# One group of gate columns moved to seven-product form, with its factors made earlier and twelve low parts made by adding transfers

## The chip, the cores and the metric

The kernel runs on one core of a Trainium2 chip. Five engines each follow an instruction list of their own: TensorE (PE, matrix products, with PEld loading its weights), VectorE (DVE), ScalarE (ACT), GpSimd (POOL) and SyncE (SP). Transfers between the main memory and the on-chip memory are issued from the queues of SP, ACT or POOL. The metric is the device time of one execution in microseconds, lower is better. Times of the kernel before: 806.62 us, the median of 3 runs (806.59 to 807.14).

## The reference

One decoder layer over 512 tokens of width 1024, in float32: a norm, one wide projection, three attention branches side by side (banded attention, called SWA; stick-breaking attention, SB; attention over 256 memory rows, MEM), each multiplied by a sigmoid gate of its own, an output projection and a gated feed-forward block.

```python
u = rms_norm(h, ln_mix_pre[l])
proj = jnp.einsum('bsd,de->bse', u, w_in[l])
qa, ka, va, qb, kb, vb, qm, gl = jnp.split(proj, split_idx, axis=-1)
...
g = jax.nn.sigmoid(gl.reshape(B, S, N_BRANCH, D))
merged = (g[:, :, 0] * jnp.einsum('bse,ed->bsd', y_swa, w_branch_swa[l])
          + g[:, :, 1] * jnp.einsum('bse,ed->bsd', y_sb, w_branch_sb[l])
          + g[:, :, 2] * jnp.einsum('bse,ed->bsd', y_mem, w_branch_mem[l]))
```

What the change touches is `gl`, the gates: three branches of 1024 columns each, computed from the normed input `u` (1024 x 512, eight row blocks of 128).

## The kernel before

**Three products for one.** Every float32 operand is split into a rounded part `hi` and the rest `lo`, and a product of two operands is three matmuls into the same bank: hi·hi, hi·lo and lo·hi (`mm3`, L167, whose matmuls are L169, L171 and L172 in the profile). `split` (L132) makes the parts: ScalarE copies the raw weights to `hi` with rounding (L135), VectorE subtracts `hi` from the raw weights to get `lo` (L136). With a sign of -1, the same two steps are L138 and L139.

**A stream of units.** The weights come through a `Stream` (L33), a list of units of 512 KB each, in the order in which they were added. Loads run four units ahead of the products and splits three units ahead (`ahead`, L58). There are five `raw` tiles and four `hi` and four `lo` tiles for all units, so the split of a unit waits until TensorE has finished the unit four places earlier. `run(us)` (L92) issues products of the stream worth so many us by a cost that is written in the code, to fill the time in which an attention head waits for VectorE and ScalarE. `until(flag)` (L97) issues them up to a mark. The instructions get their priority from the order in which the program makes them, and the compiler lays out each engine's list by that priority, taking a later instruction where an earlier one is not ready. An engine then works its list in order.

**Plain and seven-product gates.** A plain unit (`proj`, L286) is one 128-column block of the projection: 8 row blocks x 3 matmuls of 512 columns, 24 in all. Four such blocks make a group of 512 columns, and a group can also be computed with seven products of half-size blocks in place of eight (`add_quarters`, L445, `quarter`, L428), in the order p1, p2, p5, p6, p3, p7, p4, each of 24 matmuls of 256 columns. Weights of the sums are made by transfers from POOL that add to a tile in place (`q_plus`, L375) and by additions on VectorE (`q_sum`, L390). The right-hand factors are combinations of the blocks of `u`: `rights` (L457) makes those of p6, p7 and p4, and `right_t1` (L482) writes the factor of p5 over the right half of the upper blocks of `u`, so that no plain unit may follow it. Results are put together in `q_end` (L397), and the sigmoids are taken in `sigmoids` (L333) and `gate_out` (L343).

**Order before.** After the eight stick-breaking heads and the SB gates (eight plain units, mark `gates1`), the list of units goes on: four `qm` units (queries of MEM), four SB branch units (`branch`, L583), four plain SWA gate units (columns 0, 1, 4, 5, tile `g`), the mark `plain_end`, seven products for the other SWA group, four SWA branch units, and 14 products for MEM. The driver (L990 to L1006) runs four pairs of banded heads over them, then the factors, then the memory heads:

```python
for c in range(4):
    for us in swa_pair(c, bias):
        dn.run(us)
for _ in rights():
    dn.run(2.0)
dn.until("plain_end")
right_t1()
dn.until(f"gates{SWA}")
```

A pair of banded heads (`swa_pair`, L878) is a chain: scores (`s`, 16 matmuls), then 10 us asked of the stream while VectorE and ScalarE do the softmax of `w`, then 14 transposes (`pt`), 2 us of the stream while `pts` is copied, 16 matmuls of values (`ysw`), and the split of the result into `y0ch` on ScalarE and `y0cl` on VectorE.

**Tiles.** `ck` (L118) hands out 68 tiles of 128 x 512 for nearly everything else. `dps` (L124) has two banks of the matmul memory and `aps` (L127) has six.

Of the kernel before, what the change touches and what calls it, by code (L numbers as in the profile page):

```python
# [32 lines left out]
class Stream:  # L33
# [12 lines left out]
    def add(self, src, n, mm):  # L46
        self.units.append({"src": src, "n": n, "mm": mm, "load": [], "split": [], "flags": []})

    def on_load(self, fn):
        self.units[-1]["load"].append(fn)  # L50

    def on_split(self, fn):
        self.units[-1]["split"].append(fn)

    def mark(self, flag):
        self.units[-1]["flags"].append(flag)

    def ahead(self, load_to, split_to):  # L58
        while self.loaded <= min(load_to, len(self.units) - 1):
            u = self.units[self.loaded]  # L60
            for fn in u["load"]:
                fn()
            u["raw"] = u["src"]() if callable(u["src"]) else self.load(u["src"], u["n"])
            self.loaded += 1
        while self.have <= min(split_to, len(self.units) - 1):
            u = self.units[self.have]
            for fn in u["split"]:
                fn()
            u["hl"] = self.split(u["raw"], u["n"])
            self.have += 1  # L70

    def later(self, us, fn):
# [18 lines left out]

    def run(self, us):  # L92
        self.owed += us
        while self.owed > 0 and self.at < len(self.units):
            self.owed -= self.piece()

    def until(self, flag):  # L97
# [6 lines left out]
def tile_kernel(ctx, tc, a):  # L104
# [13 lines left out]
    def ck(name, dt=F32):  # L118
        return ckp.tile([P, 512], dt, tag="ck", name=name)
# [10 lines left out]
    st = {}  # L130

    def split(raw, hi, lo, sign=1.0):  # L132

        if sign == 1.0:
            ins = nc.scalar.copy(hi, raw)  # L135
            lows = nc.vector.tensor_tensor(lo, raw, hi.bitcast(F32), op=ALU.subtract)  # L136
# [8 lines left out]
    uid = [0]  # L145

    def w_load(src, n):
        uid[0] += 1
        raw = wp.tile([P, 1024], F32, tag="raw", name=f"raw{uid[0]}", bufs=5)
        nc.sync.dma_start(raw[:, :n], src)  # L150
        return raw

    def w_split(raw, n):
        uid[0] += 1
        hi = wp.tile([P, 1024], F32R, tag="hi", name=f"hi{uid[0]}", bufs=4)
        lo = wp.tile([P, 1024], F32R, tag="lo", name=f"lo{uid[0]}", bufs=4)
        sign = 1.0
# [239 lines left out]
    def q_end(b, n, p, ps):  # L397
        def done(i, f, src, sign=1.0):
            if b in st.get("sigmoid", ()):
                gate_out(b, n, i, f, src, sign)  # L400
                return
            if sign != 1.0:
                t = ck(f"qr{b}{n}")
                nc.scalar.mul(t[:, :], src[:, :], sign)
                src = t
            st.setdefault(("raw", b), []).append((n, i, f, src))

        def join(t, x, y, op, i, f):
            nc.vector.tensor_tensor(t[:, :], x[:, :], y[:, :], op=op)
            done(i, f, t)  # L410

        with tc.high_priority():
            if p in ("p1", "p5", "p6"):
                qk[p] = ck(f"qk{p}{b}{n}")
                nc.scalar.copy(qk[p][:, :], ps[:, :])
            elif p == "p3":
                t = qk.pop("p6")
                join(t, t, ps, ALU.subtract, 1, 0)
            elif p == "p7":
                t = qk.pop("p5")  # L420
                join(t, t, ps, ALU.subtract, 1, 1)
            elif p == "p2":
                t = ck(f"qj{b}{n}")
                join(t, ps, qk.pop("p1"), ALU.add, 0, 0)
            else:
                done(0, 1, ps, -1.0)

    def quarter(b, n, p):  # L428
        def gen(hi, lo):
            if p in ("p1", "p5", "p2"):  # L430
                bank = aps if b == MEM and p == "p5" else dps
                qb_[TILE[p]] = bank(f"q{TILE[p]}{b}{n}")
            ps = qb_[TILE[p]]
            for j in range(2):
                for k in range(4):
                    first = p in ("p1", "p5", "p2") and j == 0 and k == 0
                    mm3(
                        ps[:, j * 256 : (j + 1) * 256], cols((hi, lo), (j * 4 + k) * P, P), right_of(p, k), first, k == 3
                    )
                    yield 0.36  # L440
            q_end(b, n, p, ps)

        return gen

    def add_quarters(b, n):  # L445
# [5 lines left out]
        for key, what, args, back in (  # L451
# [2 lines left out]
            i = base + SEVEN.index("p5" if key == "s" else "p7") - back  # L454
            dn.units[i]["load"].append(lambda w=what, k=key, x=args: w(b, n, k, *x))

    def rights():  # L457

        names = ("p6", "p7", "p4")
        for c in range(2):  # L460
            for p in names:
                right.setdefault(p, []).append((ck(f"{p}rh{c}", F32R), ck(f"{p}rl{c}", F32R)))
            f = {p: ck(f"f{p}{c}") for p in names}
            for e in range(2):
                k, sl = 2 * c + e, slice(e * 256, (e + 1) * 256)
                x, y = ck(f"fx{k}"), ck(f"fy{k}")
                for t, j in ((x, k), (y, 4 + k)):
                    nc.vector.tensor_tensor(t[:, :], u[j][0].bitcast(F32), u[j][1].bitcast(F32), op=ALU.add)
                t1 = ck(f"ft{k}")
                one = st.setdefault("t1", {})[k] = t1[:, :256]  # L470
                nc.vector.tensor_tensor(one, x[:, 256:], x[:, :256], op=ALU.subtract)
                n2 = f["p6"][:, sl]
                nc.vector.tensor_tensor(n2, one, y[:, 256:], op=ALU.subtract)
                for p, t in (("p7", x), ("p4", y)):
                    nc.vector.scalar_tensor_tensor(f[p][:, sl], n2, -1.0, t[:, :256], op0=ALU.mult, op1=ALU.subtract)
                yield
            for p in names:
                h, l = right[p][c]
                split(f[p][:, :], h[:, :], l[:, :])
            yield  # L480

    def right_t1():  # L482

        for k, t in st["t1"].items():
            split(t, u[k][0][:, 256:], u[k][1][:, 256:])

    def val(h, q):
        def gen(hi, lo):
# [128 lines left out]
    def add_proj(kind, idx, ci):  # L617
        src = a["w_p"][:, ci].rearrange("p k n -> p (k n)")
        dn.add(src, 1024, gate(int(kind[1]), idx) if kind[0] == "g" else proj(kind, idx))

    add_proj("ka", 0, 16)
    dn.on_load(mem_load)
# [9 lines left out]
    for b, order in ((SB, 0), (SWA, 1), (MEM, 2)):  # L632
        if b == MEM:
            add_quarters(b, 0)
            add_quarters(b, 1)
        else:
            for c in range(8) if b == SB else (0, 1, 4, 5):
                add_proj(f"g{b}", c, 17 + 8 * b + c)
        if b == SWA:
            dn.mark("plain_end")  # L640
            add_quarters(b, 1)
        dn.mark(f"gates{b}")
        if b == SB:
            for i in range(4):
                add_proj("qm", i, 8 + i)
        for c2 in range(4):
            dn.add(a["w_br"][:, b, 2 * c2 : 2 * c2 + 2].rearrange("p c k n -> p (c k n)"), 1024, branch(b, c2, order))
        dn.mark(f"branch{b}")


    xraw = []
# [350 lines left out]
    table("sigmoid_and_others")  # L1002
    sigmoids(SWA)
# [604 lines left out]
```

## Time and profile before

| what | value |
|---|---|
| median of 3 runs | 806.62 us |
| profiled execution, own time | 806.6 us |
| its span, first to last instruction | 804.8 us |
| mean granted clock of TensorE | 0.998 |
| TensorE busy | 795.6 us of the span |
| VectorE busy | 616.2 us |
| ScalarE busy | 477.0 us |
| transfers | 117.68 MB, 146 GB/s mean |

The page gives for each engine its busy time, the span in 40 slices, the queues of transfers, the chain of work that ended last, and the costliest groups of instructions by line. The views of the trace used below are the list of waits of an engine, the timeline (start, duration, engine, line, operation, tiles, count, and in brackets the idle time before it with what ended it), the busy times of a stretch, and the instructions of one line with their least, median and largest duration. The duration of a matmul there includes the depth of its pipeline, so that neighbours overlap; what a matmul costs TensorE is the distance from its start to the next start. The engines overlap likewise: the next operation starts a little before the modelled end of the last one.

### The profile page before, as it was taken

The numbers are of one execution on the slowest core, as the hardware profiler recorded it, in microseconds if no ns is written. First come the engines' busy times: TensorE is split into PE (matmuls) and PEld (weight loads), VectorE is DVE, ScalarE is ACT, GpSimd is POOL, SyncE is SP. The second block draws the span as 40 slices with busy tenths as digits, with TensorE's granted clock in tenths as the row PEclk, the third lists the DMA queues.
The fourth block names the chain that finished last, engine by engine and source line by source line (L and its number), as shares of the span: only waits on it lengthen the run. The fifth ranks groups of instructions, "written<-read, shape, count | busy, mean of one in ns | idle before, by whom it ended". The sixth has DMA issues, their size and how long they took to land.

```text
span 804.8 us, 12915 instructions
## 1 busy us (share of the span) xinstructions
PE 795.6 (99%) x4939; PEld 708.2 (88%) x4939; DVE 616.2 (77%) x983; ACT 477.0 (59%) x861; POOL 78.9 (10%) x101
## 2 busy tenths in 40 slices
PE   9999999999999999999999999999999999999996
PEld 6899788878788889889988899999999999988885
DVE  6898678646377888796694779967676767898787
ACT  7466677666756555754662566554444444666673
POOL 1002210000000000100004200100000000205200
PEclk9999999999999999999999999999999999999999
DMA  9343355211241404704669927987777662859802
GB/s 320 118 148 105 125 176 149 87 53 53 80 105 53 106 26 133 182 27 132 187 234 305 224 45 172 257 222 205 190 176 191 174 167 69 190 129 225 204 2 104
DMA packets 41726, 117.68 MB, mean 146 GB/s; under 512 B 4768, under 2 KB 6320, under 8 KB 41664
## 3 DMA queue, kind: packets, MB, share of 16 engines
q1 hardware_dynamic: 31584, 87.77, 33.9%
q0 software_dynamic: 9648, 28.82, 19.2%
q8 instruction: 38, 0.62, 0.3%
q10 hardware_dynamic: 432, 0.27, 0.1%
q14 instruction: 24, 0.20, 0.1%
HBM read 113.18 MB, written 3.67 MB: 145 GB/s over the span
## 4 chain that ended last, share of the span: by engine, by line
PE 95%; DVE 2%; ACT 1%; issue 1%; DMA 1%; DVEq 0%; ACTq 0%
PE gx L172 5%; PE gx L169 5%; PE gx L171 5%; PE z L175 4%; PE g L169 3%; PE br L169 3%; PE br L171 3%; PE g L171 3%; PE g L172 3%; PE br L172 3%; PE x L172 2%; PE x L171 2%; PE x L169 2%; PE gy L171 2%; PE gy L169 2%; PE gy L172 2%
## 5 line engine op out<-in xcount | busy, mean ns | idle before, releaser
L135 ACT CAST hi<-gw 128x1024 fp32r<-128x1024 f32 x77 | 79.9, 1048 | 81.4 <-DVE gw L1193 39.8
L136 DVE TENSOR_TENSOR lo<-gw,hi 128x1024 fp32r<-128x1024 f32 x77 | 93.5, 1223 | 34.1 <-ACT hi L135 34.0
L135 ACT CAST hi<-raw 128x1024 fp32r<-128x1024 f32 (+2 forms) x52 | 53.0, 1031 | 50.8 <-PE qb L171 11.3
L136 DVE TENSOR_TENSOR lo<-raw,hi 128x1024 fp32r<-128x1024 f32 (+2 forms) x52 | 63.0, 1217 | 20.1 <-ACT hi L135 19.9
L1175 POOL DMA_DIRECT2D gw<-in_w_gu x27 | 23.3, 895 | 190.4 <-DMA gw<-in_w_gu 81.4
L135 ACT CAST hi<-r 128x1024 fp32r<-128x1024 f32 (+1 forms) x24 | 23.5, 981 | 19.9 <-PE y L172 5.3
L171 PE MATMUL x<-lo,lh 128*128 128x512 f32 x88 | 34.3, 389 | 0.0
L169 PE MATMUL x<-hi,lh 128*128 128x512 f32 x88 | 34.2, 389 | 0.0
L172 PE MATMUL x<-hi,ll 128*128 128x512 f32 x88 | 34.1, 389 | 0.0
L136 DVE TENSOR_TENSOR lo<-r,hi 128x1024 fp32r<-128x1024 f32 (+1 forms) x24 | 27.1, 1130 | 4.0 <-ACT hi L135 3.9
L135 ACT CAST hi<-qw 128x1024 fp32r<-128x1024 f32 x18 | 18.9, 1051 | 16.0 <-PE g L171 3.9
L136 DVE TENSOR_TENSOR lo<-qw,hi 128x1024 fp32r<-128x1024 f32 x18 | 21.9, 1219 | 8.4 <-ACT hi L135 8.4
L835 DVE SCALAR_TENSOR_TENSOR e<-z,e 128x384 f32<-128x384 f32 (+1 forms) x24 | 14.3, 598 | 17.7 <-ACT e L188 17.7
L188 ACT ACTIVATE e<-e 128x384 f32<-128x384 f32 (+1 forms) x48 | 26.9, 561 | 1.6
L135 ACT CAST hi<-bp 128x512 fp32r<-128x512 f32 x33 | 19.3, 620 | 13.6 <-PE y L172 4.8
L136 DVE TENSOR_TENSOR lo<-bp,hi 128x512 fp32r<-128x512 f32 x33 | 22.1, 702 | 5.7 <-ACT hi L135 5.6
L172 PE MATMUL gx<-N2h,lo 128*128 128x256 f32 x88 | 25.0, 284 | 0.3 <-DVE lo L136 0.3
L169 PE MATMUL gx<-B11h,hi 128*128 128x256 f32 x88 | 25.1, 285 | 0.2 <-ACT B11h L1104 0.2
L169 PE MATMUL mx<-woh,mgh 128*128 128x512 f32 x64 | 25.0, 391 | 0.0
L172 PE MATMUL gw<-B21h,lo 128*128 128x256 f32 x88 | 25.0, 284 | 0.0
L171 PE MATMUL gx<-B11l,hi 128*128 128x256 f32 x88 | 25.0, 284 | 0.0
L172 PE MATMUL mx<-woh,mgl 128*128 128x512 f32 x64 | 24.9, 390 | 0.0
(920 smaller groups left out, 2967.5 us busy)
## 6 DMA issues: line engine op xcount, KB each, us to landing
gw<-in_w_gu SPq DMA_DIRECT2D x57, 512.0 KB, 5.1
gw<-in_w_gu POOLq DMA_DIRECT2D x27, 512.0 KB, 7.4
raw<-in_w_p SPq DMA_DIRECT2D x26, 512.0 KB, 4.3
qw<-in_w_p SPq DMA_DIRECT2D x15, 512.0 KB, 4.1
raw<-in_w_br SPq DMA_DIRECT2D x12, 512.0 KB, 3.8
bp<-in_w_dn SPq DMA_DIRECT2D x22, 256.0 KB, 8.7
r<-in_w_dn POOLq DMA_DIRECT2D x10, 512.0 KB, 8.1
raw<-in_w_out SPq DMA_DIRECT2D x8, 512.0 KB, 4.4
```

The costliest lines, as they stand in the source:

```text
L135: ins = nc.scalar.copy(hi, raw)
L136: lows = nc.vector.tensor_tensor(lo, raw, hi.bitcast(F32), op=ALU.subtract)
L169: one = nc.tensor.matmul(out, lh, rh, start=start, stop=False, skip_group_check=True)
L171: nc.tensor.matmul(out, *two, start=False, stop=False, skip_group_check=True)
L172: return one, nc.tensor.matmul(out, *three, start=False, stop=stop, skip_group_check=True)
L175: return nc.tensor.matmul(out, l, r, start=start, stop=stop, skip_group_check=True)
L188: ins = nc.scalar.activation(*args, **kw)
L835: nc.vector.scalar_tensor_tensor(x, z[i][:, :n], 0.0, x, op0=ALU.max, op1=ALU.add)
L1175: nc.gpsimd.dma_start(gw[(n, key)][:, :], g_src(n, i, j), accum_op=ALU.add)
```

## The change

The other SWA group (columns 0, 1, 4, 5) is now computed with seven products too, and the two groups run side by side: p1 of group 0, p1 of group 1, then p5, p2, p6, p7, p3 and p4 in the same way. So each SWA group has a bank of its own for the sums, and `qk` and `qb_` are kept by branch and group. The sums of weights for p6 and p3 are made by further adding transfers (`q_plus` behind the split of p5 and of p6), no longer by `q_sum`. The order of the units after the SB gates becomes: four SB branch units, four `qm` units, `plain_end`, the 14 SWA products, four SWA branch units, MEM as before. A `gate` stops `run` at a place until `open`: one ahead of the SB branch units, and one ahead of the SWA products that opens when `rights` has written the p5 factor. `rights` now comes with the p5 factor first (in `x`, straight into `u`), then p6, then p7 and p4, in place on `x` and `y` and with its splits by halves of 256. For the four SB branch, four `qm` and four SWA branch units `lo` is made differently: ScalarE copies `hi`, ScalarE writes `-hi` into `lo`, and a POOL transfer adds the 512 KB of weights from the main memory to it once more.

```diff
+    def split_dma(raw, hi, lo, src):
+
+        nc.scalar.copy(hi, raw)
+        nc.scalar.mul(lo, hi.bitcast(F32), -1.0)
+        nc.gpsimd.dma_start(like(lo, src), src, accum_op=ALU.add)
...
     def run(self, us):
         self.owed += us
-        while self.owed > 0 and self.at < len(self.units):
+        while self.owed > 0 and self.at < len(self.units) and self.at not in self.gates[:1]:
             self.owed -= self.piece()
...
+        order = [(n, p) for p in ("p1", "p5", "p2", "p6", "p7", "p3", "p4") for n in range(2)]
...
+        for n in range(2):
+            load_with((n, "p5"), 4, q_raw, b, n, "s", 1, 0)
+            load_with((n, "p5"), 2, q_plus, b, n, "s", 1, 1)
+            load_with((n, "p7"), 4, q_raw, b, n, "t", 1, 0)
+            load_with((n, "p7"), 3, q_plus, b, n, "t", 0, 0)
+        for n in range(2):
+            for p, j in (("p5", 0), ("p6", 1)):
+                dn.units[base + order.index((n, p))]["after"].append(lambda n=n, j=j: q_plus(b, n, "s", 0, j))
...
+        for k in range(4):
+            x[k] = ck(f"fx{k}")
+            a0, a1 = x[k][:, :256], x[k][:, 256:]
+            nc.vector.tensor_tensor(x[k][:, :], u[k][0].bitcast(F32), u[k][1].bitcast(F32), op=ALU.add)
+            nc.vector.tensor_tensor(a1, a1, a0, op=ALU.subtract)
+            split(a1, u[k][0][:, 256:], u[k][1][:, 256:])
+        dn.open()
+        yield
...
+        for k in range(4):
+            y[k] = ck(f"fy{k}")
+            b1 = y[k][:, 256:]
+            nc.vector.tensor_tensor(y[k][:, :], u[4 + k][0].bitcast(F32), u[4 + k][1].bitcast(F32), op=ALU.add)
+            nc.vector.tensor_tensor(b1, x[k][:, 256:], b1, op=ALU.subtract)
+            part("p6", k, b1, 1.0)
             yield
...
+        for p, z in (("p7", x), ("p4", y)):
+            for k in range(4):
+                b0 = z[k][:, :256]
+                nc.vector.tensor_tensor(b0, y[k][:, 256:], b0, op=ALU.add)
+                part(p, k, b0, -1.0)
+                if k % 2:
+                    yield
...
+    dn.gate()
+    add_branch(SB, 0, True)
+    for i in range(4):
+        add_proj("qm", i, 8 + i, lo_by_dma=True)
+    dn.mark("plain_end")
+    dn.gate()
+    add_two_groups(SWA)
+    dn.mark(f"gates{SWA}")
+    add_branch(SWA, 1, True)
...
     sigmoids(SB)
+    dn.open()
     table("natural_log_exp_and_others")
     for c in range(4):
         for us in swa_pair(c, bias):
             dn.run(us)
+    dn.until("plain_end")
     for _ in rights():
-        dn.run(2.0)
-    dn.until("plain_end")
-    right_t1()
+        dn.run(1.5)
     dn.until(f"gates{SWA}")
```

More of the change, by code (lines that the diff above doesn't have):

```diff
@@ L44, in __init__, with add @@
         self.deferred, self.flags = [], set()
-    def add(self, src, n, mm):
-        self.units.append({"src": src, "n": n, "mm": mm, "load": [], "split": [], "flags": []})
+        self.gates = []
+    def add(self, src, n, mm, lo_by_dma=False):
+        self.units.append({"src": src, "n": n, "mm": mm, "load": [], "split": [], "flags": [], "after": [], "dma": lo_by_dma})
     def on_load(self, fn):
@@ L53, in on_split, with gate, open @@
         self.units[-1]["split"].append(fn)
+    def gate(self):
+        self.gates.append(len(self.units))
+    def open(self):
+        self.gates.pop(0)
+        self.owed = 0.0
     def mark(self, flag):
@@ L68, in ahead @@
                 fn()
-            u["hl"] = self.split(u["raw"], u["n"])
+            u["hl"] = self.split(u["raw"], u["n"], *([u["src"]] if u["dma"] else []))
+            for fn in u["after"]:
+                fn()
             self.have += 1
@@ L145, in tile_kernel, with like @@
     uid = [0]
+    def like(t, src):
+        return t.rearrange("p (g m) -> p g m", g=src.shape[1]) if len(src.shape) == 3 else t
     def w_load(src, n):
@@ L156, in w_split @@
         lo = wp.tile([P, 1024], F32R, tag="lo", name=f"lo{uid[0]}", bufs=4)
+        if src is not None:
+            split_dma(raw[:, :n], hi[:, :n], lo[:, :n], src)
+            return hi, lo
         sign = 1.0
@@ L423, in q_end @@
                 t = ck(f"qj{b}{n}")
-                join(t, ps, qk.pop("p1"), ALU.add, 0, 0)
+                join(t, ps, qk.pop((b, n, "p1")), ALU.add, 0, 0)
             else:
@@ L430, in gen @@
             if p in ("p1", "p5", "p2"):
-                bank = aps if b == MEM and p == "p5" else dps
-                qb_[TILE[p]] = bank(f"q{TILE[p]}{b}{n}")
-            ps = qb_[TILE[p]]
+                bank = aps if p == "p5" or (b, p) == (SWA, "p2") else dps
+                qb_[(b, n, TILE[p])] = bank(f"q{TILE[p]}{b}{n}")
+            ps = qb_[(b, n, TILE[p])]
             for j in range(2):
@@ L455, in add_quarters @@
             dn.units[i]["load"].append(lambda w=what, k=key, x=args: w(b, n, k, *x))
-    def rights():
[L459 to L479, printed above, removed]
-            yield
@@ L482, in right_t1, with add_two_groups, load_with @@
-    def right_t1():
-        for k, t in st["t1"].items():
-            split(t, u[k][0][:, 256:], u[k][1][:, 256:])
+    PLAIN = {"p1": (0, 0), "p2": (0, 1), "p4": (1, 1)}
+    def add_two_groups(b):
+        order = [(n, p) for p in ("p1", "p5", "p2", "p6", "p7", "p3", "p4") for n in range(2)]
+        base = len(dn.units)
+        for n, p in order:
+            if p in PLAIN:
+                dn.add(q_src(b, n, *PLAIN[p]), 1024, quarter(b, n, p))
+            else:
+                dn.add(q_got(b, n, p), 1024, quarter(b, n, p))
+        def load_with(unit, back, *args):
+            dn.units[base + order.index(unit) - back]["load"].append(lambda: args[0](*args[1:]))
+        for n in range(2):
[6 more added lines that the diff above has]
+                dn.units[base + order.index((n, p))]["after"].append(lambda n=n, j=j: q_plus(b, n, "s", 0, j))
@@ new lines, in rights, with part @@
+    def rights():
+        x, y = {}, {}
+        def part(p, k, src, sign):
+            h, l = cols(right[p][k // 2], (k % 2) * 256, 256)
+            split(src, h, l, sign)
+        for k in range(4):
[6 more added lines that the diff above has]
+        yield
+        for p in ("p6", "p7", "p4"):
+            right[p] = [(ck(f"{p}rh{c}", F32R), ck(f"{p}rl{c}", F32R)) for c in range(2)]
+        for k in range(4):
[4 more added lines that the diff above has]
+            part("p6", k, b1, 1.0)
+            yield
+        for p, z in (("p7", x), ("p4", y)):
[5 more added lines that the diff above has]
+                    yield
@@ L615, in tile_kernel, with add_proj @@
     dn.mark("sb_ready")
-    def add_proj(kind, idx, ci):
+    def add_proj(kind, idx, ci, **kw):
         src = a["w_p"][:, ci].rearrange("p k n -> p (k n)")
-        dn.add(src, 1024, gate(int(kind[1]), idx) if kind[0] == "g" else proj(kind, idx))
+        dn.add(src, 1024, gate(int(kind[1]), idx) if kind[0] == "g" else proj(kind, idx), **kw)
     add_proj("ka", 0, 16)
@@ L631, in tile_kernel, with add_branch @@
     add_proj("qa", 3, 15)
[L632 to L645, printed above, removed]
-        for c2 in range(4):
-            dn.add(a["w_br"][:, b, 2 * c2 : 2 * c2 + 2].rearrange("p c k n -> p (c k n)"), 1024, branch(b, c2, order))
-        dn.mark(f"branch{b}")
+    def add_branch(b, order, by_dma):
+        for c2 in range(4):
+            src = a["w_br"][:, b, 2 * c2 : 2 * c2 + 2].rearrange("p c k n -> p (c k n)")
+            dn.add(src, 1024, branch(b, c2, order), lo_by_dma=by_dma)
+    for c in range(8):
+        add_proj(f"g{SB}", c, 17 + 8 * SB + c)
+    dn.mark(f"gates{SB}")
+    dn.gate()
[7 more added lines that the diff above has]
+    add_branch(SWA, 1, True)
+    for n in range(2):
+        add_quarters(MEM, n)
+    dn.mark(f"gates{MEM}")
+    add_branch(MEM, 2, False)
+    dn.mark(f"branch{MEM}")
     xraw = []
```

12 lines of the change are left out of this document (6 added, 6 removed).

## The prediction

> **What bounds the kernel now.** I read the page first, then TensorE's list of waits, then its timeline around the banded heads.
>
> ```profile
> span 804.8 us, 12915 instructions
> ...
> PE 795.6 (99%) x4939; PEld 708.2 (88%) x4939; DVE 616.2 (77%) x983; ACT 477.0 (59%) x861; POOL 78.9 (10%) x101
> ...
> PEclk9999999999999999999999999999999999999999
> ...
> PE 95%; DVE 2%; ACT 1%; issue 1%; DMA 1%; DVEq 0%; ACTq 0%
> ```
>
> TensorE is busy for 99% of the span at full clock, and the chain that ended last is 95% TensorE. A busy TensorE need not be an efficient one, so the waits come next.
>
> ```profile
> PE warm L175 <- DVE idle L683: 1.4, 1, 1.4
> PE gx L172 <- DVE lo L136: 0.3, 1, 0.3
> ```
>
> These are the two longest entries of TensorE's waits (total, times, longest, in us). After the start nothing longer than 0.3 us shows. So the end is set by the sum of the matmuls, and VectorE's 77% costs nothing as long as it stays hidden. Two things can move the time: fewer matmul microseconds, or a new place where TensorE has nothing to do.
>
> **What the change removes.** Start to start in the timeline gives the price of a unit.
>
> ```profile
> 292.55 0.39 PE L169 MATMUL g<-n0h,hi 128*128 128x512 f32 x1
> ...
> 297.99 0.28 PE L169 MATMUL ms<-mks0h,qms0h 128*128 128x256 f32 x1
> ```
>
> ```profile
> 308.60 0.28 PE L169 MATMUL qw<-n4h,hi 128*128 128x256 f32 x1
> ...
> 311.48 0.28 PE L169 MATMUL qx<-p6rh,hi 128*128 128x256 f32 x1
> ```
>
> A plain gate unit, 24 matmuls of 512 columns, takes 297.99 - 292.55 = 5.44 us (0.227 each). A product unit, 24 of 256 columns, takes 311.48 - 308.60 = 2.88 us (0.12 each). Four plain units cost 21.76 us, seven products 20.16 us: **-1.60 us**. The other SWA group already had products, and the SB, `qm` and branch units only change places, so this is the whole direct gain, 0.20% of 806.6.
>
> The lo parts by transfer take twelve `lo` subtractions from VectorE and give ScalarE twelve more passes over 1024 columns.
>
> ```profile
> L135 ACT CAST hi<-raw 128x1024 fp32r<-128x1024 f32 (+2 forms) x52 | 53.0, 1031 | 50.8 <-PE qb L171 11.3
> L136 DVE TENSOR_TENSOR lo<-raw,hi 128x1024 fp32r<-128x1024 f32 (+2 forms) x52 | 63.0, 1217 | 20.1 <-ACT hi L135 19.9
> ```
>
> That is 12 x 1.2 = 14.6 us off VectorE and about 12 x 1.0 = 12.4 us onto ScalarE. Neither is on TensorE's path, so I count both at nothing; ScalarE's idle 41% covers its share. If it did not, one cast in front of a softmax would delay a pair of heads by 1.0 us.
>
> **What it adds: the p5 factor after the last pair.** Before, the plain SWA gates stood behind the heads and TensorE worked on them while VectorE made the factors. Now p1 of both groups alone is free of factors, and the pairs eat the units that stand before it. I follow the last pair.
>
> ```profile
> 272.76 0.40 PE L169 MATMUL br<-y10h,hi 128*128 128x512 f32 x1
> ...
> 283.00 1.69 PE L931 MATMUL pt<-c_ident,w 128*128 128x128 f32 x14
> 284.44 0.48 PE L169 MATMUL g<-n7h,hi 128*128 128x512 f32 x1
> ...
> 286.67 1.74 PE L175 MATMUL ysw<-pts,v_all 128*64 128x256 f32 x16
> 288.33 0.50 PE L169 MATMUL g<-n2h,hi 128*128 128x512 f32 x1
> ```
>
> ```profile
> 281.87 1.14 DVE L920 TENSOR_SCALAR w<-w,den 128x256 f32<-128x256 f32 x4
> ...
> 284.72 0.56 DVE L934 COPY pts<-pt 128x384 f32<-128x384 f32 x1 [0.21 <-PE pt L931]
> ...
> 289.07 0.69 DVE L136 TENSOR_TENSOR y03l<-ysw,y03h 128x512 fp32r<-128x512 f32 x1 [1.57 <-ACT y03h L135]
> 289.68 0.68 DVE L468 TENSOR_TENSOR fx<-n0h,n0l 128x512 f32<-128x512 f32 x1
> 290.28 0.68 DVE L468 TENSOR_TENSOR fy<-n4h,n4l 128x512 f32<-128x512 f32 x1
> 290.88 0.42 DVE L471 TENSOR_TENSOR ft<-fx 128x256 f32<-128x256 f32 x1
> ```
>
> ```profile
> 299.45 0.39 ACT L135 CAST n0h<-ft 128x256 fp32r<-128x256 f32 x1
> ```
>
> The scores end at 272.76. The softmax is done at 283.01 and `pt` starts at 283.00: the chain through VectorE and ScalarE takes 10.2 us, and it just fits under the 10 us that the program asks of the stream. `pt` costs 1.44, the copy of `pts` ends at 285.28, `ysw` costs 1.66 (288.33 - 286.67). Then VectorE waits 1.57 us for `y03h`, makes `y03l`, and only then starts the first factor sum `fx`, although its inputs, the parts of `u`, are old. I read this as an order that holds: the new tiles of the factors come after those of the last pair. The cause is not in the trace.
>
> After the change the same pair runs so. The costs written in the program (0.65 per three matmuls; requests 10, 2, 10, 2, 10, 2) take 56 of the 64 steps of the SB branch and `qm` units before the last scores. Eight steps of 3 x 0.227 are left: 5.44 us. Behind them are two p1 units, 5.76 us, which the compiler may pull ahead of `pt`, since they wait for nothing. With `pt` and `ysw` TensorE has 5.44 + 5.76 + 1.44 + 1.66 = **14.3 us** of work between the last scores and p5.
>
> The chain to p5 takes longer: softmax 10.2, `pt` 1.44, its copies 0.84 (285.28 - 284.44), `ysw` 1.66, then `y03` and the first quarter of the p5 factor. That last part is 1.35 from the end of `ysw` to `fx` (289.68 - 288.33), 0.68 for the sum, 0.42 for the difference, 0.39 for the ScalarE cast, and three handovers of about 0.12 (`y03h` starts 0.12 after `ysw`), about 3.2. The sum is **17.4 us**. So TensorE is idle for 17.4 - 14.3 = 3.1 us ahead of p5. Then p5 goes by quarters, and the p2 units, which need no factor, fill in.
>
> Bounds of this term: 0, if the compiler puts the new sums into VectorE's earlier idle time, against which stands the 1.57 us in which `fx` did not go ahead; 6.0, if TensorE's list puts p5 strictly first, so that it waits for three more quarters at 0.60 + 0.35 + 0.35 = 1.3 us less the 0.36 us of products for each (+2.8). I take 3.1.
>
> **The other factors.** The busy times of the stretch in which they were made before (PE, PEld, DVE, ACT, POOL):
>
> ```profile
> 289.60:309.00 19.40, 19.40 (x109) 17.00 (x108) 19.30 (x39) 10.83 (x19) 0.00 (x0) 1.00 0.00 1
> ```
>
> VectorE was full, 19.3 of 19.4 us. Now, from the end of `ysw` to p6, it has `y03l` 0.6, p5 and p6 factors 2 x 4 x 1.3 = 10.4, about three weight splits 3.5 and one join 0.6: 15.1 us. TensorE reaches p6 after 3.2 of waiting and four units, 14.7 us. That is even; up to 2 us could be missing. The MEM scores `ms`, 24 matmuls of 0.12 = 2.9 us, can stand in, so I take 0.
>
> **The SWA branch units by transfer.** Before them stand short units. The `lo` of the first one can start when p3 of group 0 has ended, and it is wanted three units later, 8.64 us.
>
> ```profile
> L377 POOL DMA_DIRECT2D qw<-in_w_p x6: 1194/1198/1260, 230.9 to 369.8; - x6
> ...
> DMA to landing us min/median/max: 5.9/7.5/8.6
> ```
>
> ```profile
> L1175 POOL DMA_DIRECT2D gw<-in_w_gu x27: 850/859/1193, 433.7 to 644.6; - x27
> ...
> DMA to landing us min/median/max: 5.4/7.4/13.7
> ```
>
> Two ScalarE passes 2.1, POOL 1.2 and the landing 7.5 make 10.8, so it is 2.2 us late; behind the units in the program stand `ms` with 2.9. I take 0; if `ms` was spent earlier it is +2.2, and with a landing of 13.7 it is 17.0 - 8.64 = 8.4, or 5.5 with `ms`. In the pairs the same wait has three units of 5.44 = 16.3 us, so even 17.0 costs little. POOL's list is in order: behind a waiting transfer stand the memsets of `w` and the next transfers, but in these 16 us they have room.
>
> The Trainium skill (SBUF — State Buffer, section "SBUF: two separate sides") says that a VectorE operation in a two-port mode keeps GpSimd from writing descriptors, so that such a transfer seems blocked. The landing of 5.4 to 13.7 us above is the spread beside a busy VectorE in this trace; by the rule the late end is the one to expect, and the sum would be up to 5.5 us higher. By the median row it is not.
>
> **Sum.** 806.6 - 1.6 + 3.1 = **808.1 us**. The profiled execution took 806.6 (span 804.8 and 1.8 around it), the median of the runs is 806.62, so no shift between them.
>
> **Rivals.**
> - **No new wait.** The factor sums slide into VectorE's idle time, which the moved `lo` parts enlarge. Then the gain stays: 805.0. Against it stands the place of `fx`.
> - **VectorE becomes the bound at the factors**, slower. The p5 quarters and the p6 factor come one after another and TensorE's list does not fill in: 3.1 + 2.8 + up to 2 - 1.6, or 811 to 813 at the worst, about 810.5 with half of the later terms. It decides as soon as VectorE's 15.1 us slip behind TensorE's 14.7 by more than the 2.9 us of `ms`. For it speaks the full VectorE row; against it the work taken from VectorE in the pairs.
> - **The first SWA branch unit waits for its transfer.** 2.2 to 5.5 more: 810.3 to 813.6.
> - **The wait turns the clock down.** The first matmuls of the trace are the only slow ones.
>
> ```profile
> 1.35 4.58 PE L175 MATMUL warm<-idle 128*128 128x512 bf16 x11 [1.35 <-DVE idle L683]
> ```
>
> Eleven in 4.58 us are 0.42 each against 0.227. If a wait brought that back for as long, it would cost about 4.58 x (1 - 0.227/0.42) = 2.1 us more: 810.2. It needs an unbroken wait; 3.1 us in one piece is near what might do it, broken by `pt` and `ysw` it is not. The Trainium skill (TensorE: Matmul & The Clock Gate, section "Part 1") gives half clock after an idle window of about 3.4 us; by that the forecast stays just below it, and no wait of the trace before is long enough to test it.
>
> **How the numbers follow.** Forecast (a wait of 2 to 4.5 us, 807.0 to 809.5) 0.45, of which 0.14 lies above 808.2. No new wait 0.25, of which 0.10 lies below 805.0. VectorE as the bound 0.15, the branch transfer 0.08, the clock 0.07. A measurement of this kernel tells 0.2%, 1.6 us, from no change. So: faster 0.10, same 0.31 + 0.15 = 0.46, slower 0.14 + 0.15 + 0.08 + 0.07 = 0.44. The range reaches from the full gain, 805.0, to 811.0, which leaves out the worst of the three slower cases.
>
> **What would show it.** Right: TensorE idle for about 3 us, put down to VectorE or ScalarE writing `n0h` to `n3l`, just ahead of the `qy` matmuls; `fx` behind `y03l`; VectorE full for 15 us after that. Four `g` units gone and 14 products of 2.88. Wrong: `fx` ahead of `y03l`, or no wait at `qy`; or waits at `br` on the adding transfer, or a granted clock below 1 there; or a softmax chain far from 10.2 us now that ScalarE has two more passes for each unit.

## The result, and the profile after

The kernel after the change takes 817.22 us (median of 4 runs, 815.13 to 819.57) against 806.75 us before (4 runs, 806.59 to 807.14): a ratio of 1.013, 95% interval 1.0102 to 1.0158. It is slower by 10.5 us. The prediction was 808.1 us with a range up to 811.0, so the time lies outside the range, on the side that it gave 0.44.

The profiled execution took 817.39 us. From its page, the span, the busy times, the granted clock in 40 slices and the chain that ended last:

```profile
span 815.6 us, 13121 instructions
...
PE 797.2 (98%) x5011; PEld 713.3 (87%) x5011; DVE 607.5 (74%) x981; ACT 491.5 (60%) x886; POOL 96.7 (12%) x119
...
PEclk9999999999999999999999999999999999999999
...
PE 92%; DMA 3%; DVE 2%; ACT 1%; issue 1%; DVEq 0%; POOL 0%; ACTq 0%; POOLq 0%
```

The page hardly shows what happened. VectorE has 8.7 us less work than before and ScalarE 14.5 us more (the prediction had 14.6 less and 12.4 more); TensorE's share is 98% in place of 99%, and DMA has gone from 1% to 3% of the chain. TensorE's busy time even grew by 1.6 us, although 1.6 us of matmuls were taken away: a TensorE at half clock, whose matmuls start about twice as far apart, counts as busy too. The list of TensorE's waits (total, times, longest, in us) has two new entries at its head:

```profile
PE br L195 <- DMA lo<-in_w_br: 5.3, 2, 3.4
PE qy L192 <- ACT n0h L146: 2.9, 1, 2.9
```

**The wait ahead of p5.** TensorE's timeline there (start, duration, engine, line, operation, tiles, count, idle time before with its releaser), then VectorE's at the same place:

```profile
288.31 0.28 PE L195 MATMUL qx<-n3h,lo 128*128 128x256 f32 x1
291.53 0.80 PE L192 MATMUL qy<-n0h,hi 128*128 128x256 f32 x2 [2.94 <-ACT n0h L146]
292.13 0.41 PE L192 MATMUL qw<-n4h,hi 128*128 128x256 f32 x1
292.34 0.41 PE L194 MATMUL qw<-n4l,hi 128*128 128x256 f32 x1
...
294.47 0.33 PE L194 MATMUL qy<-n0l,hi 128*128 128x256 f32 x1
```

```profile
288.81 0.69 DVE L147 TENSOR_TENSOR y03l<-ysw,y03h 128x512 fp32r<-128x512 f32 x1 [1.56 <-ACT y03h L146]
289.42 0.68 DVE L515 TENSOR_TENSOR fx<-n0h,n0l 128x512 f32<-128x512 f32 x1
```

The last matmul of p1 starts at 288.31, the first of p5 at 291.53: 3.22 us start to start where 0.12 is due, so 3.10 us are lost. `fx` stands directly behind `y03l`, as it did before, behind 1.56 us of idle time (1.57 before). Behind the wait the next matmuls start 0.21 us apart and not 0.12, until 294.65; 14 of them take 3.12 us for 1.68, which is another 1.4 us. This is the half clock: the granted clock of the stretch from 284 to 304 us is 0.91.

**Two waits in the SWA branch.** The same view of TensorE, later:

```profile
330.62 0.40 PE L194 MATMUL br<-y00l,hi 128*128 128x512 f32 x1
332.97 0.50 PE L195 MATMUL br<-y00h,lo 128*128 128x512 f32 x1 [1.95 <-DMA lo<-in_w_br]
...
338.32 0.39 PE L194 MATMUL br<-y00l,hi 128*128 128x512 f32 x1
342.08 0.57 PE L195 MATMUL br<-y00h,lo 128*128 128x512 f32 x1 [3.37 <-DMA lo<-in_w_br]
342.44 0.63 PE L192 MATMUL br<-y01h,hi 128*128 128x512 f32 x1
342.87 0.63 PE L194 MATMUL br<-y01l,hi 128*128 128x512 f32 x1
```

Each time the two products with `hi` start and the third, with `lo`, waits for the adding transfer. The first two branch units are each late: 2.35 - 0.23 = 2.12 us and 3.76 - 0.23 = 3.53 us. Behind the second the matmuls start 0.43 us apart until 345.82, where 0.227 is due: 9 of them in 3.74 us for 2.04, so 1.7 us more. After the first, shorter wait they go on at 0.23.

Where the transfers were held up is in the timelines of GpSimd (three rows) and of ScalarE (one row):

```profile
322.71 0.90 POOL L171 DMA_DIRECT2D lo<-in_w_br x1 [1.32 <-ACT lo L170]
333.35 1.20 POOL L400 DMA_DIRECT2D qw<-in_w_p x1 [9.73 <-DMA qw<-in_w_p]
334.06 2.31 POOL L171 DMA_DIRECT2D lo<-in_w_br x2
```

```profile
324.24 1.06 ACT L170 ACTIVATE lo<-hi 128x1024 fp32r<-128x1024 f32 x1
```

Unit 0's transfer goes out at 322.71 and has landed when TensorE goes on at 332.97, ten us later. Unit 1's `-hi` is written at 325.30, but its transfer goes out after 334.06: ahead of it in GpSimd's list stands the transfer that adds up a weight sum for MEM, and that one sits for 9.73 us until its own raw weights have come. The view of the transfers between 300 and 345 us (packets, MB, share of 16 engines; then the issues with their median us to landing) shows how full the 16 engines that move the data were:

```profile
q0 software_dynamic: 1646, 3.93, 50.4%
q1 hardware_dynamic: 2215, 5.25, 33.8%
...
qw<-in_w_p SPq DMA_DIRECT2D x5, 512.0 KB, 8.3
...
lo<-in_w_br POOLq DMA_DIRECT2D x4, 512.0 KB, 9.8
```

The two queues fill 84% of the 16 engines in this stretch, and the median landing is 9.8 us, where the prediction took 7.5. While unit 0's transfer was under way, the busy times (PE, PEld, DVE, ACT, POOL, then granted clock, share of the transfer engines, GB/s) were:

```profile
322.70:333.00 10.30, 8.35 (x69) 7.92 (x67) 1.55 (x3) 8.69 (x16) 0.90 (x1) 1.00 1.02 264
```

The transfer engines were busy throughout, and VectorE for 1.55 of 10.30 us only. So a busy VectorE, which the prediction named as a reason for a late landing, was not there; that full engines are the reason fits, but no run empties them at this place to show it.

**The sum.** 806.6 - 1.6 (seven products) + 3.1 (p5) + 1.4 (half clock behind it) + 2.1 and 3.5 (SWA branch) + 1.7 (half clock behind the second) = 816.8, against 817.39 measured for this execution. The remaining 0.6 us are not accounted for one by one; an early wait for `uh` is 1.0 us in this list, 0.2 in that of the kernel before and not in e1's, so it varies between executions.

### The profile page after: what moved, and what is told of

Same layout as the page of the kernel before. It is cut to its first block, busy times and chain, and to the rows that moved or that the text cites. A ratio compares the mean times of both kernels' runs of the same rounds, so it can differ in the third digit from the quotient of the medians.

```text
span 815.6 us, 13121 instructions
## 1 busy us (share of the span) xinstructions
PE 797.2 (98%) x5011; PEld 713.3 (87%) x5011; DVE 607.5 (74%) x981; ACT 491.5 (60%) x886; POOL 96.7 (12%) x119
## 4 chain that ended last, share of the span: by engine, by line
PE 92%; DMA 3%; DVE 2%; ACT 1%; issue 1%; DVEq 0%; POOL 0%; ACTq 0%; POOLq 0%
PE gx L195 5%; PE gx L192 5%; PE gx L194 5%; PE z L198 3%; PE br L195 3%; PE br L192 3%; PE br L194 2%; PE x L195 2%; PE x L194 2%; PE x L192 2%; PE gy L195 2%; PE gy L194 2%; PE gy L192 2%; PE g L192 2%; PE g L194 2%; PE mx L192 2%
## 5 line engine op out<-in xcount | busy, mean ns | idle before, releaser
L146 ACT CAST hi<-raw 128x1024 fp32r<-128x1024 f32 (+2 forms) x42 | 42.5, 1025 | 32.6 <-PE qb L194 11.3
L147 DVE TENSOR_TENSOR lo<-raw,hi 128x1024 fp32r<-128x1024 f32 (+2 forms) x42 | 50.9, 1215 | 9.7 <-ACT hi L146 9.6
L400 POOL DMA_DIRECT2D qw<-in_w_p x12 | 14.6, 1245 | 114.4 <-DVE lo L147 49.0
L643 DVE TENSOR_TENSOR g<-br,g 128x512 f32<-128x512 f32 x24 | 16.5, 688 | 15.4 <-PE br L195 15.3
```

The lines of the kernel that those rows point to most:

```text
L400: nc.gpsimd.dma_start(raw[:, :].rearrange("p (g m) -> p g m", g=2), q_src(b, n, f, j), accum_op=ALU.add)
L643: nc.vector.tensor_tensor(g[:, :], ps[:, :], g[:, :], op=ALU.mult)
```

## The experiments

In all, "before" is the kernel before, run on the same chip beside the experiment. In e1 to e3 and e5 to e12 the edit is to the kernel after the change, in e4 to the kernel before.

**e1: no transfers in the SWA branch.**

```diff
-    add_branch(SWA, 1, True)
+    add_branch(SWA, 1, False)
```

> The changed kernel, but the four SWA branch units get their lo part by the subtraction on VectorE again. Theory (two places with a wait, each with slow-clock matmuls behind it): the changed kernel is 806.6 - 1.6 (products) + about 3.0 (wait ahead of p5) + 1.7 (matmuls at 0.21 in place of 0.12 after it) + 5.3 (waits of the SWA branch units for their adding transfers) + 1.6 (slow clock after the second of them) = 816.6. Without the transfers there the last two terms go: about 810, with the wait ahead of p5 unchanged at 2.9. Rival (POOL and the DMA engines are overfull in this stretch whatever the branch units do, because of the eight further adding transfers of the weight sums): the wait moves to p6, p3 or the MEM products, and the time stays above 814.

Measured 809.84 us (10 runs, 808.39 to 810.91), ratio 1.0035 (1.0026 to 1.0044). The one large wait left in TensorE's list:

```profile
PE qy L192 <- ACT n0h L146: 2.9, 1, 2.9
```

So the four transfers in the SWA branch cost 817.2 - 809.8 = 7.4 us, which agrees with 2.1 + 3.5 + 1.7 = 7.3 of the trace. What stays is near the forecast of 808.1: the shortest execution, the profiled one, took 808.39, the median is 1.7 us above the forecast (e6 says why).

**e4: the transfers alone**, in the same twelve units of the kernel before, with its own order and gates.

```diff
-            u["hl"] = self.split(u["raw"], u["n"])
+            u["hl"] = self.split(u["raw"], u["n"], *([u["src"]] if u["dma"] else []))
...
+            nc.scalar.copy(hi[:, :n], raw[:, :n])
+            nc.scalar.mul(lo[:, :n], hi[:, :n].bitcast(F32), -1.0)
+            nc.gpsimd.dma_start(lo[:, :n], src, accum_op=ALU.add)
```

> The kernel before with one part of the change alone: lo by adding transfer in the same twelve units (four qm, four SB branch, four SWA branch), the order and the gates as before. Theory: nothing in the pairs of heads, where a unit has 16 us for its lo, and a wait at the SWA branch, behind the short products: 806.6 + 2 to 4, no wait elsewhere. Rival (the transfers add freely and only the other products around them make them late): 806.6, no wait at br. Second rival (two more ScalarE passes lengthen the softmax chains): waits at pt in the pairs, up to 1 us each.

Measured 814.14 us (4 runs), ratio 1.009 (1.0075 to 1.0105): a loss of 7.3 us without any change of the gates, larger than expected. The head of its waits:

```profile
PE br L177 <- DMA lo<-in_w_br: 4.8, 1, 4.8
```

That is again the SWA branch, here one wait of 4.8 us: unit 0's transfer goes out at 321.12, and TensorE goes on at 329.91, 8.8 us later. The granted clock from 324 to 344 us is 0.91, so half clock is part of the loss. There is no wait at the eight units beside the pairs of heads. So it is the place that makes these transfers dear, not the form of the split.

**e5: the two groups with no transfer for `lo` anywhere.**

```diff
-    add_branch(SB, 0, True)
+    add_branch(SB, 0, False)
...
-        add_proj("qm", i, 8 + i, lo_by_dma=True)
+        add_proj("qm", i, 8 + i)
...
-    add_branch(SWA, 1, True)
+    add_branch(SWA, 1, False)
```

> The changed kernel with no lo part by transfer at all (SB branch and qm units on VectorE too), so the two groups side by side, the order and the early factors alone. Theory: the subtractions taken from VectorE in the pairs of heads hide nothing that is late, so the time is that of the run with only the SWA branch units put back, 808.4 to 810.9, with the wait of 2.9 us at qy. Rival (the freed VectorE shortens the softmax chains, and without it the last pair ends later): the wait at qy grows by 1 us or more, and waits show at pt: 811 or more.

Measured 810.89 us (4 runs), ratio 1.0047 (1.0032 to 1.0062), against e1's 1.0035 (1.0026 to 1.0044). The medians differ by 1 us and the intervals overlap, so no gain of the eight transfers that are left in e1 is shown. Their profiled executions differ in the clock. The stretch 284 to 304 us (busy times of PE, PEld, DVE, ACT, POOL, then granted clock, share of the transfer engines, GB/s), e1 first, then e5:

```profile
284.00:304.00 20.00, 17.06 (x141) 16.24 (x140) 18.25 (x39) 12.70 (x25) 2.29 (x2) 1.00 0.37 84
```

```profile
284.00:304.00 20.00, 17.06 (x119) 16.33 (x118) 16.43 (x33) 10.02 (x18) 1.83 (x2) 0.83 0.32 80
```

Both have the wait of 2.9 us, but only e5's record shows a lower clock behind it.

**e6: the wait ahead of p5 filled.** e1, with twelve matmuls of zeros into p5's bank ahead of its first product.

```diff
+            if (b, n, p) == (SWA, 0, "p5"):
+                for _ in range(12):
+                    mm(ps[:, :], idle[:, :P], idle[:, :], True, True)
...
-    add_branch(SWA, 1, True)
+    add_branch(SWA, 1, False)
```

> The kernel with the SWA branch units put back to VectorE, with twelve further matmuls of zeros (512 columns, bf16, 2.6 us) into p5's own bank ahead of p5 of group 0, where TensorE waits 2.9 us; p5 then overwrites the bank. Theory (the wait is 2.9 us in every run, and in some runs the clock drops behind it): the wait is filled, the clock stays, all runs lie near 808.4 to 809.0, against 808.4 to 810.9 without. Rival (the spread has another source): the same spread, median near 809.8, or 2.6 us more if the wait were not there.

Measured 808.48 us (10 runs, 808.21 to 808.87), ratio 1.0017 (1.0007 to 1.0026). All ten runs lie within 0.7 us, where e1's lie within 2.5. The matmuls do nothing useful; what they take away is the spread above 808.9. The spread alone would not prove it, since the kernel before, run beside e6, spread from 806.16 to 808.76. The granted clock of the runs does: its mean is 0.995 to 0.997 in the seven runs of e1 above 809 us, and 0.997 to 0.999 in the other three and in all ten of e6. So the half clock behind this wait is real, comes in some executions and not in others, and is worth up to 2 us.

**e2: p2 ahead of p5**, so that work without a factor stands in the wait.

```diff
-        order = [(n, p) for p in ("p1", "p5", "p2", "p6", "p7", "p3", "p4") for n in range(2)]
+        order = [(n, p) for p in ("p1", "p2", "p5", "p6", "p7", "p3", "p4") for n in range(2)]
```

> The changed kernel with p2 ahead of p5 in the order of the products, since p2 needs no factor. Theory: 5.76 us of products now cover the 2.9 us ahead of p5, so the wait at qy and the slow matmuls behind it go: 817.2 - 4.6 = 812.6, with the waits at br unchanged. Rival (VectorE is the bound from there on): the wait comes back at p5 or p6, since p6 now starts right behind p5, and less than 2 us are gained: 815 or more.

Measured 822.54 us (4 runs), ratio 1.0186 (1.0166 to 1.0207): a miss, and the slowest of all. The two waits at the head of its list:

```profile
PE br L195 <- DMA lo<-in_w_br: 7.5, 2, 4.5
PE qx L192 <- ACT hi L146: 2.8, 1, 2.8
```

The wait at `qy` is gone, and one of 2.8 us stands at p6: the sum of its weights is a transfer that starts only behind the split of p5, and p5 now comes closer to p6. The branch waits grew from 5.3 to 7.5 us.

**e3: e1 and e2 together.**

> Both edits together. Theory: what is left is the seven-product gain, 806.6 - 1.6 = 805.0, up to 1 us more for p6 waiting for its sum, so 805 to 806, not slower than before. Rival (the factors or the sums by transfer are the bound): 808 or more, with waits at p6, p7 or p3.

Measured 812.42 us (4 runs), ratio 1.0067 (1.0052 to 1.0082), a miss too, with one large wait left:

```profile
PE qx L192 <- ACT hi L146: 2.9, 1, 2.9
```

ScalarE's row ahead of it is a cast of the weight sum that itself waited for the adding transfer:

```profile
304.71 1.99 ACT L146 CAST hi<-qw 128x1024 fp32r<-128x1024 f32 x2 [3.16 <-DMA qw<-in_w_p]
```

So covering p5's wait this way moves the whole of it to p6, two products later, and half clock comes behind it (granted 0.91 from 304 to 324 us).

**e7: only group 0's p2 ahead of p5**, and e1's branch.

```diff
+        order = [(0, "p1"), (1, "p1"), (0, "p2"), (0, "p5"), (1, "p5"), (1, "p2")]
+        order += [(n, p) for p in ("p6", "p7", "p3", "p4") for n in range(2)]
```

> The kernel with the SWA branch units put back to VectorE, and p2 of group 0 moved ahead of the two p5, p2 of group 1 left between p5 and p6. Theory: 2.88 us of products cover the 2.9 us ahead of p5, and one unit still stands between p5 and p6, against none when both p2 were moved (a wait of 2.9 us at p6 then, for the sum that a transfer makes from p5's weights): 805.0 to 806.0. Rival (the sum needs both units between): a wait at p6 of 2 us or more, 807 to 810.

Measured 808.66 us (10 runs, 807.61 to 809.46), ratio 1.0015 (1.0006 to 1.0025). Better than e1 and short of what was expected: the wait at `qy` is gone, 1.2 us come back at p6, and 0.7 us stand in the MEM heads.

```profile
PE qx L195 <- DVE lo L147: 1.2, 1, 1.2
PE mpt L1031 <- DVE mw L1025: 0.7, 1, 0.7
```

**e8: a request of 9 in place of 10** in each pair of heads, which leaves more of the stream for the end, and e1's branch.

```diff
-        yield 10.0
+        yield 9.0
```

> The kernel with the SWA branch units put back to VectorE, and 9 us in place of 10 asked of the stream for a softmax, so that five steps of three matmuls (3.4 us) move behind the last scores. Theory: the wait at qy goes from 2.9 to about 0, as long as the softmax still fits under the shorter request: 805.0 to 806.5. Rival (the first pairs need the 10 us): waits of about 1 us at pt in two pairs, and the gain ahead of p5 is given back: 807.5 to 809.5.

Measured 809.62 us (7 runs), ratio 1.0029 (1.0017 to 1.004). A miss: p5 no longer waits, but 0.4 us come back at p3, 0.7 at p7 and 0.7 in MEM's gates at 382, the last two for the join `qkp` of VectorE and ScalarE. These are 1.8 us; the rest of the distance to 805 us is not accounted for.

**e9: the sums earlier.** e1, with the four sums `fx` and their differences made ahead of the last pair; only the splits into `n0h` to `n3l` stay behind it.

```diff
             nc.vector.tensor_tensor(a1, a1, a0, op=ALU.subtract)
-            split(a1, u[k][0][:, 256:], u[k][1][:, 256:])
+        yield
+        for k in range(4): split(x[k][:, 256:], u[k][0][:, 256:], u[k][1][:, 256:])
...
+    made = rights()
     for c in range(4):
+        if c == 3: next(made)
         for us in swa_pair(c, bias):
             dn.run(us)
```

> e1 (branch units of SWA without transfers) with the four sums fx and their differences made ahead of the last pair instead of behind it; what is left behind the last qm unit is the split into n0h to n3l. Theory (the 2.9 us ahead of p5 is the place of the sums in VectorE's list, and the 3.8 us they take there also make p6 late in e3, e7 and e8): both waits go, no single wait over 0.5 us at qy or qx, 806.7 - 1.6 + about 0.5 = 805 to 806. Rival (VectorE is full throughout, so work put earlier only makes the last softmax late): pt or qy waits 1 to 3 us, 808 to 810.

Measured 812.34 us (5 runs, 811.23 to 812.43), ratio 1.0057 (1.0043 to 1.0071): the theory's number fell, the rival's side held, and by more than it said. VectorE's timeline shows the place:

```profile
272.00 0.69 DVE L147 TENSOR_TENSOR y02l<-ysw,y02h 128x512 fp32r<-128x512 f32 x1 [0.22 <-ACT y02h L146]
272.61 0.68 DVE L514 TENSOR_TENSOR fx<-n0h,n0l 128x512 f32<-128x512 f32 x1
...
276.36 0.29 DVE L953 TENSOR_TENSOR w<-s,bias 128x128 f32<-128x128 f32 x1
```

`fx` now stands directly behind the `y02l` of the pair before, and the last softmax, whose scores TensorE began at 271.27, starts at 276.36, 3.75 us later than `fx`. In e1 it starts at 272.60. The wait at `qy` is gone, but TensorE now waits twice ahead of p1, for a copy that ScalarE makes amid the late softmax, and p5 itself starts at 294.47 in place of 291.22 in e1:

```profile
PE qx L192 <- ACT qm L327: 3.3, 2, 1.7
```

**e11: the sums under the pair before the last.** As e9, asked for between that pair's transposes and its values.

```diff
-        if c == 3: next(made)
         for us in swa_pair(c, bias):
+            if (c, us) == (2, 2.0): next(made)
```

> As e9_sums_early, but the four sums fx and their differences are asked for between the transposes and the values of the pair before the last, so that VectorE has them in its list ahead of y02l and not between y02l and the last softmax. Theory (VectorE has no room left in the last pair, but some in the pair before): most of the 3.8 us go under that pair, the four splits n0l to n3l (4 x 0.35) still stand in the last softmax; pt and p5 one to two us late in all, 807 to 809, below e9's 811 to 812. Rival (place does nothing, VectorE is full in each pair): 810 to 812.

Measured 810.2 us (5 runs, 808.95 to 810.63), ratio 1.004 (1.0026 to 1.0053): between the two, nearer to the rival. p5 now follows p1 without a wait, at 288.75, and the loss is one step on, at p7:

```profile
PE qx L192 <- ACT qkp L438: 2.0, 1, 2.0
```

The copy that it waits for stands in ScalarE's list behind a cast of a weight sum, and that cast waited for the sum's adding transfer:

```profile
310.12 1.06 ACT L149 ACTIVATE hi<-qw 128x1024 fp32r<-128x1024 f32 x1 [3.61 <-DMA qw<-in_w_p]
311.08 0.57 ACT L438 COPY qkp<-qx 128x512 f32<-128x512 f32 x1
```

Behind this wait of 2.02 us the matmuls start 0.21 us apart from 312.76 to 316.17, so half clock came here too: 16 of them in 3.41 us for 1.92.

**e12: the sums on GpSimd.** As e11, the eight operations on another engine.

```diff
-            nc.vector.tensor_tensor(x[k][:, :], u[k][0].bitcast(F32), u[k][1].bitcast(F32), op=ALU.add)
-            nc.vector.tensor_tensor(a1, a1, a0, op=ALU.subtract)
+            nc.gpsimd.tensor_tensor(x[k][:, :], u[k][0].bitcast(F32), u[k][1].bitcast(F32), op=ALU.add)
+            nc.gpsimd.tensor_tensor(a1, a1, a0, op=ALU.subtract)
```

> As e11_sums_in_pair2, with the four sums and four differences on GpSimd in place of VectorE: 3.8 us off VectorE, 4 x 1.4 + 4 x about 0.8 = 9 us onto GpSimd, which has 15.8 us of idle time there in e1. Theory (VectorE's work is what binds in the last pair and at p6): no wait over 0.6 us at qy or qx, 805 to 806.5. Rival (GpSimd's list takes its place: the memsets of the last pair's w and the adding transfer of a weight sum stand behind the eight operations): 1 to 4 us late at s, pt or qy, 807 to 810.

Measured 815.64 us (4 runs), ratio 1.0108 (1.0094 to 1.0122): both theory and rival fell. GpSimd's list was in time, the memsets too. The loss is on VectorE, whose softmax comes late; the longest entry of TensorE's waits, then one row of e11's VectorE timeline, then e12's, then GpSimd's in e12:

```profile
PE pt L986 <- DVE w L975: 3.7, 2, 2.0
```

```profile
257.35 0.22 DVE L966 TENSOR_SCALAR nm<-nm,sinks 128x4 f32<-128x4 f32 x1
```

```profile
257.12 0.28 DVE L953 TENSOR_TENSOR w<-s,bias 128x128 f32<-128x128 f32 x1
257.32 6.50 DVE L966 TENSOR_SCALAR nm<-nm,sinks 128x4 f32<-128x4 f32 x1
263.73 0.41 DVE L954 TENSOR_TENSOR w<-s,bias 128x256 f32<-128x256 f32 x1
```

```profile
255.50 1.79 POOL L514 TENSOR_TENSOR fx<-n0h,n0l 128x512 f32<-128x512 f32 x1
...
261.90 1.88 POOL L515 TENSOR_TENSOR fx<-fx 128x256 f32<-128x256 f32 x2
```

An operation on 128x4 elements that takes 0.22 us in e11 takes 6.50 in e12, and ends when GpSimd's last sum does (261.90 + 1.88 = 263.78). The next step of that softmax starts at 263.73 and not at 257.48, as in e11: 6.25 us late.

**e10: the order on GpSimd.** The kernel after the change, with MEM's second weight sum of group 0 put behind the transfers of the branch units.

```diff
+        if (b, n, key) == (MEM, 0, "t"): after(ins, st["lod"][-2])
```

Here `st["lod"]` lists the adding transfers for `lo`, and `after` only fixes an order. (In the expectation "unit 2's wait" is the second wait, which the rows above show to be that of unit 1.)

> The changed kernel with one order added on POOL: the adding transfer of MEM's second weight sum (group 0), which stood ahead of those of SWA branch units 1 and 2 and waited for its raw weights until 333.35, now comes behind them. Theory (unit 2's wait of 3.4 us is that queue, unit 0's of 2.0 us is the landing): the second wait at br and the half clock behind it go, 3.4 + 1.7, the first stays: about 812. Rival (the transfer engines are full, the order on POOL does nothing): both waits at br stay, 816 or more.

Measured 813.06 us (4 runs, 811.11 to 815.23), ratio 1.0073 (1.0053 to 1.0093). GpSimd's timeline and the waits at `br`:

```profile
323.87 0.90 POOL L171 DMA_DIRECT2D lo<-in_w_br x1 [1.00 <-ACT lo L170]
326.74 0.86 POOL L171 DMA_DIRECT2D lo<-in_w_br x1 [1.98 <-ACT lo L170]
329.97 0.86 POOL L171 DMA_DIRECT2D lo<-in_w_br x1 [2.37 <-ACT lo L170]
333.26 1.20 POOL L400 DMA_DIRECT2D qw<-in_w_p x1 [2.43 <-DMA qw<-in_w_p]
```

```profile
PE br L195 <- DMA lo<-in_w_br: 2.2, 1, 2.2
```

Each branch transfer now goes out as soon as its `-hi` is written, and of the two waits the second is gone, the first about as before (2.19 us against 1.95): 4.2 us of the 5.1 that were expected. So the order of GpSimd's list made the second wait. The first is the landing itself: 323.87 to 334.37 in this run, again some ten us. The four runs go from 811.11 to 815.23 us as their mean granted clock goes from 0.997 down to 0.991. The profiled one is the longest, and in it the matmuls behind the wait of 2.19 us start 0.43 us apart from 334.96 to 338.36, which those behind the 1.95 us of the kernel after the change did not.

None of the twelve beats the kernel before. Nearest are e6 and e7 at 0.15 to 0.17% above it.

## Why the prediction was wrong, step by step

**The direct gain, -1.60: holds.** TensorE has 72 matmuls more (5011 against 4939), as 168 of 256 columns in place of 96 of 512 make. With the wait ahead of p5 as the only other change that a trace shows, e6's 808.48 is 806.8 - 1.6 + 3.1 to within 0.2.

**The wait ahead of p5, +3.1: right in place and cause, and in size partly by luck.** 3.10 us, released by `n0h`, with `fx` behind `y03l`. TensorE's side came as worked out: eight steps of `qm` and two p1 units stood between the last scores and p5. VectorE's side did not. The scores ended at 273.57, and the transposes were through at 282.51, 8.9 us later, where 10.2 + 1.44 = 11.6 were forecast. The copies of `pts` then stood behind other work, so that `ysw` began 3.65 us after the transposes and not 0.84:

```profile
281.94 0.82 PE L986 MATMUL pt<-c_ident,w 128*128 128x128 f32 x6
285.10 1.01 DVE L989 COPY pts<-pt 128x384 f32<-128x384 f32 x2
286.16 2.00 PE L198 MATMUL ysw<-pts,v_all 128*64 128x256 f32 x16
```

The two errors cancel to 0.1 us. e1, which has this wait and not those of the branch, ran from 808.4 up. Why the sums don't go earlier was left open; e9 and e11 show them following in VectorE's list whatever they are written behind.

**The step that failed: "The SWA branch units by transfer", of which the prediction said "I take 0".** It was worth +2.1, +3.5 and 1.7 of half clock, 7.3 us by the trace and 7.4 by e1. Three parts of its working were off. It saw one unit late, and two are. It set `ms` (2.9 us) against the first unit's lateness, and about half of those matmuls had been spent already, since only 1.6 of their 2.9 us stand between the last matmul of p4 and `br`. And it took the landing from the weight sums of the kernel before and from a later stage, 7.5 in the middle, where in this stretch it is ten, with the transfer engines full and VectorE nearly idle. The rival for it (0.08, up to 5.5 us for one unit) had the mechanism; 7.3 is above its upper end.

**What stood behind the waiting transfer.** The prediction looked at GpSimd's list in the pairs, and found memsets with room. It didn't follow the same list into the SWA branch, where a weight sum for MEM stood ahead of unit 1 and waited 9.73 us for SyncE's load. e10 removes that one thing and gets 4.2 us back.

**The clock.** The rival had 0.07 and 2.1 us, "near what might do it". It came behind both long waits: 1.4 and 1.7 us. After 2.94 us of waiting the clock is at half in the trace after, in e5 and in e10, and not in e1. Shorter waits did it too: 2.19 us in e10, 2.02 in e11, and in e9 the second of two waits of 1.59 and 1.68 us, but not the 1.95 of the kernel after the change. The Trainium skill (TensorE: Matmul & The Clock Gate, section "Part 1") speaks of an idle window of about 3.4 us that runs free of the program. That it comes and goes from run to run fits a window of its own; that 2.02 us were enough does not fit a full idle window of 3.4, and there the measurement decides.

**The other factors, 0: right only behind the wait.** In the kernel after the change nothing over 0.3 us waits at p6 or p7, because p5's wait gives VectorE and the transfers that time. Wherever p5's wait is covered, something comes back at p6 or p7: 2.9 us (e3), 1.2 (e7), 0.7 (e8), 2.0 (e11). So the rival "VectorE becomes the bound" is one of two next limits behind the forecast. In e7 that is shown: `hi` of the late weight was there by 302.23, and VectorE, without a pause, came to its `lo` only at 305.85; in e2, e3 and e11 it is the weight sum, since ScalarE there waits for the transfer that makes it. Which of the two binds in e8 is open.

**Twelve `lo` parts off VectorE, counted at nothing: right for eight of them as far as the runs tell.** e5 against e1 shows no gain clear of the spread.

## What to carry to other kernels

When a step on an idle engine becomes a transfer, price it at its place: the slot from free buffer to first use, how full the transfer engines are in that stretch, and everything that stands ahead of it in the issuing engine's list, with what that waits for in turn. A product form that needs prepared factors saves TensorE time only if other TensorE work stays to cover the preparation; here the plain units that it replaced had been that cover, and each reordering that took the wait away brought waits elsewhere. Allow for half clock behind any wait of 2 us or more: here it came in some executions and not in others, at about 1.4 to 1.7 us each time.

## What the runs showed of the hardware

- **Adding transfers take twice the engine time.** Between 300 and 345 us the adding queue used 50.4% of the engines for 3.93 MB, the plain one 33.8% for 5.25 MB: 12.8 against 6.4 points for each MB. In the kernel before, with the engines less full, the same stretch has 22.2% for 1.57 MB and 31.4% for 4.72 MB: 14.1 against 6.7.
- **A tiny VectorE operation can be stopped by a row of GpSimd's.** In e12 a TENSOR_SCALAR on 128x4 stood for 6.50 us and ended with the last of GpSimd's eight sums, while TENSOR_TENSOR and TENSOR_REDUCE just ahead of it ran beside those sums at their usual 0.28 and 0.64 us. The Trainium skill (SBUF — State Buffer, section "SBUF: two separate sides") describes a pair of ports that VectorE in a two-port mode and GpSimd lock against each other for one instruction. The trace agrees that one of the two stands still; it shows it standing through the rest of a series of eight, not through one instruction. That these ports are the cause is not shown.
